# A decoder layer on one core: gathered rows in the output weights' place, and the selection's bias on GpSimd

## The chip, the cores and the metric

The kernel runs on 1 core of one Trainium2 chip. The metric is the device time of one execution in microseconds; before the change it is 1406.47 us, the median of 3 runs (1405.79 to 1407.11).

## The reference, cut to what matters

One layer of a hybrid decoder for 1024 prompt tokens and 32 sample tokens (8 sequences of 4, each with 1024 cached positions), all in float32. All 1056 tokens share the weights.

```
xn   = rms_norm(x);  q, k, v, index q/k/weights = split(xn @ w_in)
a    = sparse attention: score = sum_h iw_h * relu(iq_h . ik); the 256 best keys of each query; softmax over them alone
b    = differential attention: (softmax(q1 k1) - lam * softmax(q2 k2)) @ v
h    = x + concat(a, rms_norm(b) * 0.2) @ w_out
y    = h + MoE(rms_norm(h)):  4 groups x 8 experts; the best group, in it the best 2 experts;
       each expert  (silu(x w_g) * (x w_u) * gate) @ w_d   with w_g, w_u 1024x256 and w_d 256x1024
```

For the sparse attention the kernel must mark for every query exactly 256 keys, with ties at the threshold decided by the lower position, as `top_k` does. For the experts it must add, for each token, two experts' results to `h`.

## The kernel before, in words

The kernel is written with a framework that traces instructions from Python, gives tiles of pools their places, sets all waits, and orders the instructions of each engine by a planner's costs; `mix` interleaves two streams of work by hand-written costs (the numbers that they yield). `V`, `S`, `G`, `T_`, `Y` are VectorE, ScalarE (ACT), GpSimd (POOL), TensorE and SyncE (SP, the queue of plain DMAs). A pool closed and another opened gives its memory on, and a tile of the new pool waits for the tiles that lay in its place (`reuse_waits="tile"`). `tc.issue_after(ins)` puts instructions behind `ins` on its engine.

1. *Projection* (to about 470 us). Six sections of `w_in` on TensorE, each over eight tiles of 128 tokens. Beside it `selection` runs (`score_tile`, `sample_index`, `select`). `select` has seven jobs: query tiles 2 to 7 (widths 384 to 1024) and the 32 sample tokens (width 1056). A bisection and an exact step give each row its threshold `Tv` and the count `need` of entries equal to it that still belong to the 256. Then for each job ACT writes the signs of score minus threshold (L697), VectorE marks the zeros among them (L698), sums them along the row (scan, L699) and compares (L700), which marks what is left out and counts it, and ACT multiplies the marks by 1e30 into the bias tile (L701). `bad` compares the counts with what they should be (L706), and `select_end` has an exact path that is taken only if one differs. The attention reads the bias.
2. *Attention* (to about 920 us), prompt and samples interleaved.
3. *Output projection and routing* (to about 1072 us). `project` multiplies the mixed heads by `w_out`, held as a high and a low part: `woh` and `wol`, 64 KB of each partition on the right side. Its last work on POOL is the power of L1344. `route` finds experts and slots. The list `it0` of an early group, made from what was routed so far, lets experts 0 to 3 begin (`xg0s`, `gu0`, `hid`, `yo0`); the lists `its` of groups 1 to 23 come when all tokens are routed (L1444, L1445).
4. *Experts*. Each group has 128 slots in 4 units of 32 rows; an expert has 96 slots, so it fills three units. For group `g`: `fetch` gathers 128 rows of the stored `h` with an indirect DMA of POOL (L1449); `turn_rows` transposes them on TensorE into two PSUM buffers, which VectorE empties with a multiply (L1458, L1459); `turned_hidden` transposes the hidden rows of the group before (L1478, L1479); `first_products` multiplies by gate and up weights (L1466), four units side by side on TensorE; `gated` applies the silu (L1470, L1472); `down` does the second products of the group before (L1486), ACT writes the result tile `yo` (L1620), and `add_rows` adds it to the output rows with an indirect accumulating DMA of POOL (L1489). Each scatter waits for the one before it, since they write one tensor.

The weights come through SP, in the order of their first use (`weights`, L1253): gate and up together 2 MB (`wg`), down 1 MB (`wd`) for each of 32 experts. There are places for 6 experts of each: four in `xw`, two in `xw2`, which opens in the place of `wol` and the second half of `woh` when the last projection tile begins. A load into a place waits until the products that read it are done. The first load of each kind behind the early ones (`HOLD`) also waits for a copy from `its` on POOL, so that it does not go too early. `ep`, the groups' pool, opens in the place of the routing's pools `fp` and `sm` once these are closed: six row tiles `xg`, each cleared by VectorE before its first gather since a gather skips empty slots, and four result tiles `yo`.

PSUM has eight banks. For the groups `psum(2)` gives two buffers to the transposes (`tr`), two to the first products (`acc`) and two double banks to the second (`S`).

## Time and profile before

| | us |
|---|---|
| median of the runs shown | 1406.47 |
| the profiled execution | 1398.5 |
| its span, first to last instruction | 1396.7 |
| TensorE, VectorE, ACT, POOL busy | 1258.1, 801.4, 561.7, 447.7 |

The page shows the busy share of each engine, the span in slices, and groups of instructions by line. Finer views of the same execution are a timeline by engine, waits by line (who waited for whom, in total), and windows (busy time of each engine in a stretch, with TensorE's granted clock as a share of full speed, the busy share of the DMA engines and the GB/s moved). `PEld` is TensorE's weight load, `SPq` the issue of DMAs on SP; in a timeline the bracket behind a row is the idle time of that engine ahead of it and what ended it. Line numbers are those of the kernel before.

### The profile page before, as it was taken

How to read it: one execution, taken by the hardware profiler on the slowest of the kernel's cores; microseconds unless marked ns; L12 is line 12 of the kernel's file. 1: busy time of each engine (PE TensorE's matmuls, PEld its weight loads, DVE VectorE, ACT ScalarE, POOL GpSimd, SP SyncE). 2: the span in 40 equal slices, each digit the busy share in tenths (PEclk: the TensorE clock that was granted, in tenths of full speed). 3: DMA queues.
4: the chain of work that ended last, by engine and by line, in shares of the span. 5: the costliest groups of instructions: out<-in, count | busy, mean ns of one | idle time of the engine just before them, and what ended most of it. 6: DMA issues, size and time to landing. Idle time of an engine off the chain costs nothing. (4 is left out here: it accounts for less than half of the span.)

```text
span 1396.7 us, 24892 instructions
## 1 busy us (share of the span) xinstructions
PE 1258.1 (90%) x9393; PEld 842.8 (60%) x9393; DVE 801.4 (57%) x2232; ACT 561.7 (40%) x1240; POOL 447.7 (32%) x505
## 2 busy tenths in 40 slices
PE   7999999997789689898889989999998799999994
PEld 5877675875467576675675776768884233333331
DVE  5545996969987677676655556836653311122210
ACT  5533666895432365544445555722221011111110
POOL 1012233254336534335237644322121212222101
PEclk9999999998899799999999999999999899999997
DMA  7223004133325865666558653357636699999962
GB/s 245 68 90 123 25 24 121 48 110 74 99 98 142 233 245 214 232 212 234 178 199 283 222 167 129 92 188 289 248 117 229 235 386 396 396 389 384 391 216 36
DMA packets 114294, 272.60 MB, mean 195 GB/s; under 512 B 52600, under 2 KB 52856, under 8 KB 101880
## 3 DMA queue, kind: packets, MB, share of 16 engines
q1 hardware_dynamic: 81248, 180.84, 35.5%
q0 software_dynamic: 26272, 87.58, 20.0%
q10 hardware_dynamic: 6648, 2.54, 0.7%
q8 instruction: 75, 1.23, 0.3%
q14 instruction: 51, 0.42, 0.1%
HBM read 234.33 MB, written 44.44 MB: 200 GB/s over the span
## 5 line engine op out<-in xcount | busy, mean ns | idle before, releaser
L532 PE MATMUL acc<-wh,xh 128*128 128x512 f32 x432 | 174.6, 404 | 13.8 <-ACT wh L508 13.8
L533 PE MATMUL acc<-wh,xl 128*128 128x512 f32 x432 | 172.0, 398 | 0.0
L1466 PE MATMUL acc<-wg,xT 128*32 128x512 f32 x1472 | 164.3, 598 | 0.0
L941 ACT ACTIVATE mk<-mk,mx 128x256 f32<-128x256 f32 (+7 forms) x128 | 99.0, 774 | 83.2 <-DVE mx L939 78.8
L535 PE MATMUL acc<-wl,xh 128*128 128x512 f32 x320 | 126.5, 395 | 0.0
L1472 DVE SCALAR_TENSOR_TENSOR ac<-acc,its,sg 128x256 f32<-128x256 f32 x23 | 15.8, 688 | 165.1 <-ACT sg L1470 165.1
L532 PEld LDWEIGHTS acc<-wh,xh 128*128 128x128 f32 x432 | 82.5, 191 | 46.3 <-ACT wh L508 22.1
L1466 PEld LDWEIGHTS acc<-wg,xT 128*32 128x32 f32 x1472 | 45.6, 110 | 101.8 <-issue 101.5
L533 PEld LDWEIGHTS acc<-wh,xl 128*128 128x128 f32 x432 | 82.5, 191 | 17.3 <-issue 1.2
L1470 ACT ACTIVATE sg<-acc,its 128x256 f32<-128x256 f32 x23 | 10.9, 473 | 194.7 <-PE acc L1466 194.7
L1486 PE MATMUL S<-wd,aTe 128*32 128x512 f32 x736 | 83.2, 592 | 0.6 <-DVE aTe L1479 0.6
L1105 PE MATMUL tr<-cst,pg 128*128 128x128 f32 x512 | 78.9, 287 | 0.5 <-DVE ql L407 0.4
L937 PE MATMUL tr<-KS,qh 128*128 128x512 f32 (+3 forms) x192 | 74.0, 390 | 1.5 <-DVE aT L865 0.7
L959 POOL TENSOR_SCALAR mk<-mk,rl 128x128 f32<-128x128 f32 (+7 forms) x64 | 49.1, 780 | 69.2 <-DVE rl L951 64.1
L1449 POOL DMA_INDIRECT xg<-s_hn,its x23 | 23.5, 1022 | 140.3 <-PE tr L1458 122.8
L877 PE MATMUL tr<-cst,mk 128*128 128x128 f32 x432 | 64.9, 281 | 3.9 <-POOL mk L959 2.4
L535 PEld LDWEIGHTS acc<-wl,xh 128*128 128x128 f32 x320 | 60.7, 190 | 11.7
L1489 POOL DMA_INDIRECT out_o_y_dram<-yo,its x23 | 36.2, 1576 | 91.7 <-ACT yo L1620 52.1
L1105 PEld LDWEIGHTS tr<-cst,pg 128*128 128x128 f32 x512 | 61.6, 147 | 6.4 <-issue 1.2
L938 PE MATMUL tr<-KS,ql 128*128 128x512 f32 (+3 forms) x192 | 65.1, 353 | 0.0
L1459 DVE TENSOR_TENSOR xT<-tr,gc 128x512 f32<-128x512 f32 x46 | 29.7, 686 | 60.6 <-PE tr L1458 60.6
L877 PEld LDWEIGHTS tr<-cst,mk 128*128 128x128 f32 x432 | 48.5, 142 | 21.8 <-issue 13.5
(447 smaller groups left out, 2913.9 us busy)
## 6 DMA issues: line engine op xcount, KB each, us to landing
wg<-in_w_exp_gate_dram SPq DMA_DIRECT2D x32, 1024.0 KB
wg<-in_w_exp_up_dram SPq DMA_DIRECT2D x32, 1024.0 KB
wd<-in_w_exp_down_dram SPq DMA_DIRECT2D x32, 1024.0 KB
wr<-in_w_in_dram SPq DMA_DIRECT2D x56, 256.0 KB
xt<-in_x_prompt_dram SPq DMA_DIRECT2D x16, 512.0 KB
s_mix<-mo SPq DMA_DIRECT2D x16, 256.0 KB
qn<-s_qa SPq DMA_DIRECT2D x8, 512.0 KB
raw<-in_w_out_dram SPq DMA_DIRECT2D x16, 256.0 KB
```

The source lines that it names most:

```text
L532: T_.matmul(ps, lhsT=xh[t][:, kc, :], rhs=wh[kc], start=kc == 0 and t < NT - 1, stop=False)
L533: T_.matmul(ps, lhsT=xl[t][:, kc, :], rhs=wh[kc], start=False, stop=t == NT - 1 and kc == KC - 1)
L535: T_.matmul(ps, lhsT=xh[t][:, kc, :], rhs=wl[kc], start=False, stop=kc == KC - 1)
L877: T_.transpose(pt[:, (j - b) * P:(j - b + 1) * P], src[:, j * P:(j + 1) * P], ident)
L937: T_.matmul(sp[:, :c1 - c0], lhsT=T.qh[:, h * P:(h + 1) * P], rhs=KS[:, h, c0:c1], start=True, stop=False)
L938: T_.matmul(sp[:, :c1 - c0], lhsT=T.ql[:, h * P:(h + 1) * P], rhs=KS[:, h, c0:c1], start=False, stop=True)
L941: S.activation(mk[:, :W], mk[:, :W], AF.Exp, bias=mx[:, h:h + 1], scale=-1.0, accum_out=T.ll[:, h:h + 1])
L959: G.tensor_scalar(ex[s][:, :W], ex[s][:, :W], T.rl[:, 2 * u + s:2 * u + s + 1], 1.0, op0=ALU.mult, op1=ALU.mult)
L1105: T_.transpose(pt[:, c * P:(c + 1) * P], raws[bb][:, o_:o_ + P], ident)
L1466: T_.matmul(gu[c:c + m, :].rearrange("p (u f) -> p u f", u=2), lhsT=xT[:, k, c:c + m], rhs=wg[:, :, k, :], start=k == 0, stop=k == KC - 1)
L1486: T_.matmul(py[q][c:c + m], lhsT=aT[:, k, c:c + m], rhs=wd[:, k, q * 512:(q + 1) * 512], start=k == 0, stop=k == 1)
L1489: G.indirect_dma_start(out=yd, out_offset=bass.IndirectOffsetOnAxis(ap=it[:, 0:1], axis=0), in_=yo, in_offset=None, compute_op=ALU.add, bo ...
```

## The change

The selection: the zeros among the signs are no longer marked by VectorE; ACT squares the signs (0 for equal, 1 else), and the scan adds a tile of ones and subtracts the squares. The last multiply goes from ACT to GpSimd.

The experts: the row tiles `xg` get a pool of their own, `xg`, on the right side under `xw2`, where the first half of `woh` lay (16 KB, four tiles), open since the last projection tile. The first two are cleared by GpSimd behind the last power, before the lists are known. `ep` keeps two result tiles in place of four, and has a third place for gate and up weights beyond the six. The loads of gate and up of experts 5 and 6 are asked for right behind the first two gathers. `hid` and `yo0` of the early group use another tag of the same pool. PSUM has three buffers for transposes and one for the first products.

```diff
@@ -690,15 +690,18 @@
         V.tensor_reduce(out=need, in_=m8, axis=AX.X, op=ALU.add)
         V.scalar_tensor_tensor(need, ge, 1.0, need, op0=ALU.add, op1=ALU.subtract)
         V.tensor_copy(cnt, thr[:, 2, :nj])
+        unit = sx.tile([P, 1056], BF16, name="unit", bufs=1)
+        G.memset(unit, 1.0)
         V.tensor_scalar(nhi, Tv, -1.0, None, op0=ALU.mult)
         for j, (sc, n, W, bt) in enumerate(J):

             sg, e = junk(), junk()
             S.activation(sg[:n, :W], sc[:n], AF.Sign, bias=nhi[:n, j:j + 1])
-            V.tensor_scalar(e[:n, :W], sg[:n, :W], 0.0, None, op0=ALU.is_equal)
-            V.tensor_tensor_scan(out=e[:n, :W], data0=e[:n, :W], data1=e[:n, :W], initial=0.0, op0=ALU.add, op1=ALU.bypass)
+            S.activation(e[:n, :W], sg[:n, :W], AF.Square)
+
+            V.tensor_tensor_scan(out=e[:n, :W], data0=unit[:n, :W], data1=e[:n, :W], initial=0.0, op0=ALU.add, op1=ALU.subtract)
             V.scalar_tensor_tensor(e[:n, :W], e[:n, :W], need[:n, j:j + 1], sg[:n, :W], op0=ALU.is_gt, op1=ALU.is_gt, accum_out=cnt[:n, j:j + 1])
-            S.mul(bt[:n, :W], e[:n, :W], BIG)
+            G.tensor_scalar(bt[:n, :W], e[:n, :W], BIG, None, op0=ALU.mult)
             yield W * 0.0035

         bad = sx.tile([P, 8], F32, name="bad", bufs=1)
@@ -1242,11 +1245,11 @@
     p4 = ExitStack()
     cq = p4.enter_context(tc.tile_pool(name="cq", bufs=1))
     xw = p4.enter_context(tc.tile_pool(name="xw", bufs=1, reuse_waits="tile"))
-    WG, WD = (4, 6), (4, 6)
+    WG, WD = (4, 6, 7), (4, 6, 6)
     xw2 = []
     NEARLY = ((1, 4), (1, 5), (0, 4))
     HOLD = (1, 1)
-    XG, YO = 6, 4
+    XG, YO = 4, 2
     SPREAD = (1, 1, 2, 3, 4, 4, 6, 6)
     loaded = [0, 0]

@@ -1255,8 +1258,8 @@
         n = loaded[part]
         loaded[part] += 1
         lim = (WG, WD)[part]
-        first = n % lim[1] < lim[0]
-        pool, bufs = (xw, lim[0]) if first else (xw2[0], lim[1] - lim[0])
+        i = n % lim[2]
+        pool, bufs = (xw, lim[0]) if i < lim[0] else (xw2[0], lim[1] - lim[0]) if i < lim[1] else (xw2[2], lim[2] - lim[1])

         def src(nm):
             return a[nm][0, e] if isinstance(e, int) else a[nm][0, bass.ds(e, 1)].rearrange("o k n -> (o k) n")
@@ -1341,7 +1344,9 @@
             st.dma_start(dst[r0:r0 + n], h[:n])
         V.tensor_tensor(out=s1[:n, 0:1], in0=s1[:n, 0:1], in1=s1[:n, 1:2], op=ALU.add)
         V.tensor_scalar(s1[:n, 1:2], s1[:n, 0:1], 1.0 / D, EPS, op0=ALU.mult, op1=ALU.add)
-        G.tensor_tensor(out=s1[:n, 2:3], in0=s1[:n, 1:2], in1=nhalf[:n, 0:1], op=ALU.pow)
+        last_pow[0] = G.tensor_tensor(out=s1[:n, 2:3], in0=s1[:n, 1:2], in1=nhalf[:n, 0:1], op=ALU.pow).ins
+
+    last_pow = [None]

     def route(t, h, s1):

@@ -1542,11 +1547,17 @@

             p3w.close()
             xw2.append(p4.enter_context(tc.tile_pool(name="xw2", bufs=1, side="right", reuse_waits="tile")))
+            xw2.append(p4.enter_context(tc.tile_pool(name="xg", bufs=XG, side="right", reuse_waits="tile")))
             for part, e in NEARLY:
                 W_[(part, e)] = weights(8 * (e % 4) + e // 4, part)
         for part, e in ahead.get(i, ()):
             W_[(part, e)] = weights(8 * e, part)

+    with tc.issue_after(last_pow[0]):
+        xgs = []
+        for _ in range(2):
+            xgs.append(xw2[1].tile([P, D], F32, name="xg"))
+            G.memset(xgs[-1], 0.0)
     step(route_)
     x0T = turn_rows(xg0s[0], lambda: fp.tile([P, KC, P], F32, name="mx"))
     step(route_)
@@ -1578,27 +1589,34 @@
     cnti = cq.tile([P, 2], I32, name="cnti")
     V.tensor_scalar(cnti[:, 0:1], cnt[:, 32:33], float(P - 1 - CAP), None, op0=ALU.add)
     V.tensor_scalar(cnti[:, 1:2], cnti[:, 0:1], 7, None, op0=ALU.arith_shift_right)
-    hid = fp.tile([P, D], F32, name="xt")
+    hid = fp.tile([P, D], F32, name="mh")
     gated(it0[:, 0], gu0, hid[:, :256], hid[:, 256:512])
     aT0 = hid[:, 512:768].rearrange("p (k n) -> p k n", k=2)
     turn_hidden(hid[:, 256:512], aT0)
     py0 = [acc(), acc()]
     second_products(py0, aT0, u0)
-    yo0 = fp.tile([P, D], F32, name="xt")
+    yo0 = fp.tile([P, D], F32, name="mh")
     for q in range(2):
         S.activation(yo0[:, q * 512:(q + 1) * 512], py0[q], AF.Copy, scale=it0[:, 0, 1:2].bitcast(F32))
     p3.close()


-    psum(2)
+    psum(3, 1)
     ep = p4.enter_context(tc.tile_pool(name="ep", bufs=2, reuse_waits="tile"))

     def fetch(it, new=False):
-        xg = ep.tile([P, D], F32, name="xg", bufs=XG)
-        if new:
-            V.memset(xg, 0.0)
+        if xgs:
+            xg = xgs.pop(0)
+        else:
+            xg = xw2[1].tile([P, D], F32, name="xg")
+            if new:
+                G.memset(xg, 0.0)
         fetch_to(it, xg)
         return it, xg
+
+
+    yos = [ep.tile([P, D], F32, name="yo", bufs=YO)]
+    xw2.append(ep)

     def new_xT():
         return ep.tile([P, KC, P], F32, name="xT")
@@ -1616,7 +1634,7 @@
     def down(it, aT, units):
         py = big()
         second_products([py[:, :512], py[:, 512:]], aT, units)
-        yo = ep.tile([P, D], F32, name="yo", bufs=YO)
+        yo = yos.pop() if yos else ep.tile([P, D], F32, name="yo", bufs=YO)
         S.activation(yo, py, AF.Copy, scale=it[:, 1:2].bitcast(F32))
         add_rows(it, yo)

@@ -1638,6 +1656,8 @@
         return units

     fetched = {g: fetch(its[:, g], True) for g in (1, 2)}
+    W_[(0, 5)], W_[(0, 6)] = (weights(8 * (n % 4) + n // 4, 0, its[:, 1, 0:1] if n == 5 else None) for n in (5, 6))
+    held[0] -= 1
     add_rows(it0[:, 0], yo0)
     behind = None
     for g in range(1, NG + 2):
...
```

What is left out at the end are the row tiles of the overflow path, renamed in the same way; that path is not taken here.

## Rows read from the trace of the kernel before

**Rows 1.** The page: engine shares, and TensorE's busy tenths in 40 slices.
```profile
PE 1258.1 (90%) x9393; PEld 842.8 (60%) x9393; DVE 801.4 (57%) x2232; ACT 561.7 (40%) x1240; POOL 447.7 (32%) x505
...
PE   7999999997789689898889989999998799999994
```

**Rows 2.** Windows: length, PE, PEld, DVE, ACT, POOL busy, granted clock, DMA share, GB/s.
```profile
1070.00:1080.00 10.00, 5.48 (x86) 2.10 (x80) 2.08 (x9) 1.85 (x3) 1.47 (x2) 1.00 0.53 211
1080.00:1090.00 10.00, 0.00 (x0) 0.00 (x0) 3.86 (x5) 0.00 (x0) 2.61 (x4) 0.64 0.43 74
1090.00:1100.00 10.00, 8.78 (x60) 3.40 (x64) 3.00 (x4) 0.00 (x0) 4.83 (x5) 0.68 0.70 215
...
1102.00:1340.00 238.00, 230.80 (x2048) 81.18 (x2051) 46.52 (x80) 30.54 (x39) 46.73 (x36) 1.00 1.01 387
```

**Rows 3.** Timeline, all engines, from the slot lists to group 2: start, us, instruction.
```profile
1071.88 0.19 POOL L1272 CAST wg<-its 128x1 f32<-128x1 int32 x1 [10.97 <-DVE its L1445]
...
1074.03 3.64 PE L1486 MATMUL acc<-wd,xt 128*32 128x512 f32 x32 [0.52 <-DVE xt L1479]
...
1078.72 1.71 POOL L1489 DMA_INDIRECT out_o_y_dram<-xt,it  x1 [6.65 <-ACT xt L1589]
1085.49 0.91 DVE L1599 MEMSET xg<- 128x1024 f32 x1 [11.52 <-DMA out_o_y_dram<-xt,it]
...
1087.20 1.06 POOL L1449 DMA_INDIRECT xg<-s_hn,its  x1 [6.78 <-DVE xg L1599]
...
1091.22 1.97 PE L1458 MATMUL tr<-cst,xg 128*128 128x128 f32 x8 [13.55 <-DMA xg<-s_hn,its]
...
1101.74 1.16 PE L1458 MATMUL tr<-cst,xg 128*128 128x128 f32 x8
```

**Rows 4.** Timeline of late groups: transposes, first products, and the readers of `acc`.
```profile
1337.42 0.44 PE L1478 MATMUL tr<-cst,ac 128*128 128x128 f32 x2 [0.34 <-DVE xT L1459]
...
1337.79 7.07 PE L1466 MATMUL acc<-wg,xT 128*32 128x512 f32 x64
...
1345.43 0.68 DVE L1472 SCALAR_TENSOR_TENSOR ac<-acc,its,sg 128x256 f32<-128x256 f32 x1 [7.12 <-ACT sg L1470]
1348.22 1.16 PE L1458 MATMUL tr<-cst,xg 128*128 128x128 f32 x8
...
1362.39 7.07 PE L1466 MATMUL acc<-wg,xT 128*32 128x512 f32 x64
```

**Rows 5.** TensorE's waits from 1100 to 1377: us in total, times, longest.
```profile
PE tr L1478 <- DVE xT L1459: 7.5, 21, 0.8
```

**Rows 6.** Window of the selection's last part, columns as in rows 2.
```profile
340.00:390.00 50.00, 32.19 (x100) 19.27 (x101) 48.07 (x91) 22.68 (x39) 17.24 (x15) 0.77 0.35 92
```

**Rows 7.** TensorE's waits from 340 to 390.
```profile
PE tr L708 <- DVE bad L706: 4.2, 1, 4.2
```

**Rows 8.** POOL's groups of instructions by shape: busy us, mean ns, idle before.
```profile
L959 POOL TENSOR_SCALAR mk<-mk,rl 128x1024 f32<-128x1024 f32 x8 | 8.9, 1120 | 13.1 <-DVE rl L951 8.5 <-PE tr L938 3.1 <-PE tr L877 1.5
...
L1084 POOL MEMSET QB<- 128x1024 f32 x2 | 1.9, 962 | 1.7 <-PE tr L1121 1.7
```

**Rows 9.** POOL's timeline: two scatters in a row in the full stretch.
```profile
1277.51 1.59 POOL L1489 DMA_INDIRECT out_o_y_dram<-yo,its  x1 [0.65 <-issue]
...
1290.81 1.59 POOL L1489 DMA_INDIRECT out_o_y_dram<-yo,its  x1 [1.64 <-DMA out_o_y_dram<-yo,its]
```

**Rows 10.** VectorE's groups of instructions from 340 to 390: the compares.
```profile
L698 DVE TENSOR_SCALAR sjunk<-sjunk 128x384 bf16<-128x384 bf16 (+6 forms) x7 | 4.5, 641 | 0.3 <-ACT sjunk L697 0.3
```

**Rows 11.** VectorE's timeline: two of the compares, of widths 896 and 1024.
```profile
350.06 1.46 DVE L698 TENSOR_SCALAR sjunk<-sjunk 128x896 bf16<-128x896 bf16 x1
...
359.38 0.42 DVE L698 TENSOR_SCALAR sjunk<-sjunk 128x1024 bf16<-128x1024 bf16 x1
```

**Rows 12.** SP's timeline: the first weight load after the pause, and the last.
```profile
1101.85 0.33 SPq L1274 DMA_DIRECT2D wg<-in_w_exp_gate_dram  x1
...
1336.02 0.33 SPq L1267 DMA_DIRECT2D wd<-in_w_exp_down_dram  x1
```

More of the change, by code (lines that the diff above doesn't have):

```diff
@@ L1661, in build @@
         nrow = 32 * OVF
-        ini = ep.tile([P, D], F32, name="xg", bufs=XG)[:, :3 * (nrow // P)].bitcast(I32).rearrange("p (i c) -> p i c", c=3)
+        ini = xw2[1].tile([P, D], F32, name="xg")[:, :3 * (nrow // P)].bitcast(I32).rearrange("p (i c) -> p i c", c=3)
         G.iota(ini[:, :, 0], pattern=[[1, nrow // P]], base=0, channel_multiplier=nrow // P)
         V.tensor_scalar(ini[:, :, 0], ini[:, :, 0], 127, None, op0=ALU.bitwise_and)
-        inif = ep.tile([P, D], F32, name="xg", bufs=XG)[:, :nrow // P]
+        inif = xw2[1].tile([P, D], F32, name="xg")[:, :nrow // P]
         V.tensor_scalar(inif, ini[:, :, 0], float(NTOK), None, op0=ALU.add)
```

## The prediction

> **What bounds the kernel now.** I read the page's engine shares first: TensorE is busy 90% of the span, so time is gained where it stands still or waits, and only there. Its busy tenths in 40 slices of 34.9 us show two dents near the lines of the diff, slices 9 and 10 (counted from 0; about 340 to 390 us) and 30 and 31 (about 1070 to 1100 us), and after them one long full stretch, the expert groups [rows 1]. I cut these stretches into windows, and then read the timeline inside them.
>
> The hole at 1080: in 1070 to 1080 TensorE is busy 5.48 of 10 us, in 1080 to 1090 not at all, and from 1080 to 1100 the granted clock is 0.64 and 0.68 of 2.4 GHz, a mix of its two levels, 1.2 and 2.4 GHz [rows 2]. The timeline says why. The slot lists `its` are done at 1071.88 (they release the POOL cast), but the gather of the first group's rows goes out at 1087.20, since its tile must be cleared first by VectorE (1085.49), in memory that the first result `yo0` still holds until its scatter, issued at 1078.72, has landed. TensorE finishes the early group at 1074.03 + 3.64 = 1077.67 and starts group 1 at 1091.22 [rows 3].
>
> The expert groups after that: from 1102 to 1340 TensorE is busy 230.8 of 238 us and the DMA share is 1.01 at 387 GB/s [rows 2]. Both are full. Which of them ends last is read from the cadence: groups follow each other every 12.30 us without exception, and the only wait that TensorE has in them is one of 0.34 us per group, of the transposes of the hidden rows (L1478) for VectorE to empty a PSUM buffer (L1459), 7.5 us in 21 waits [rows 4, 5]. No wait for weights ends last, so TensorE's own order sets the pace; the weights are near behind.
>
> The selection at 340 to 390: TensorE is busy 32.19 of 50 us there, VectorE 48.07 [rows 6]. VectorE is the bound, and TensorE's last wait in it is 4.2 us for `bad`, the end of the selection [rows 7].
>
> **The change, part by part.**
>
> *A, gathered rows in the output weights' place.* The two first row tiles now lie where the first 16 KB of `woh` lay, whose last reader is the first half of the last tile's projection, and GpSimd clears them after the last power (L1344), in a stretch in which POOL is idle for 10.97 us before the cast [rows 3]. Two GpSimd clears of this size cost 2 x 0.96 us [rows 8], hidden in that idle time; without that cover they would cost 1.9. The gathers can then go right after the cast, at 1072.1. A gather on a lightly used DMA took 1091.22 - 1087.20 = 4.0 us; the dearest nearest row is a scatter in the full stretch, 1277.51 to 1290.81 = 13.3 us [rows 3, 9]. At 1072 one 2 MB weight load (expert 5's, which that cast releases) runs beside it, a state near the light end, so I take 7 us: landed at 1079. TensorE is free at 1077.67, so group 1 starts at 1079 in place of 1091.22: 12.2 us. Group 1 before, from its first transpose to the next group's, took 1101.74 - 1091.22 = 10.5 us, at the lower clock; a later group, which also transposes hidden rows, takes from 1335.9 (12.30 before 1348.22) to the end of its first products, 1337.79 + 7.07 = 1344.9, 8.9 us, or 8.0 without the 0.34 and about 0.5 for that transpose [rows 3, 4]. With a pause of 1.3 us in place of 13.6 I expect the clock to stay up: 2.5 us more. A = 14.7 us; bounds 16.0 (no pause) and 5.8 (a 13.3 us gather, slow clock as before).
>
> What queues behind: on POOL the scatter of `yo0` follows the two gathers, is ready only at 1078, and waits for neither. On SP the two gate/up loads of experts 5 and 6 stand ahead of all others; the one for 6 goes to a new third place that lies over `yo0`, so it blocks SP until about 1086, but the next load could not go before the first products of group 1 release a place, at about 1087. It costs nothing.
>
> *B, PSUM.* `psum(3, 1)` gives the transposes a third buffer and takes one from the first products. The hidden transposes no longer wait for the buffer of L1459 and run inside the time in which the first products wait for that same evacuation anyway. 0.34 us per group, 21 times, is 7.5 us [rows 4, 5]. The first products have one buffer now: it is free when VectorE's L1472 ends (1345.43 + 0.68), and is wanted after the next row transposes, 1348.22, so 2.1 us stay in hand [rows 4]. The late one next is the evacuation L1459 itself, which the products need. B = 7.5, bounds 0 and 7.5.
>
> *C, the selection.* Out: seven compares on VectorE, 4.5 us in all. ACT's seven multiplies go to GpSimd; ACT gets seven squares of the same widths in their place, so its sum stays, and its waits for VectorE go [rows 10]. The scan and the final compare stay on VectorE, on the same number of inputs. GpSimd gets seven multiplies; a one-input multiply of 128x1024 f32 took it 1.12 us, so at most 7.8 us, and one clear [rows 8]. They hide in POOL's idle time, but VectorE, which is full, pays where the two get in each other's way: the compare of 128x896 took 1.46 us and the wider one of 128x1024 0.42 [rows 11]. Bounds: +4.5 us if nothing collides, 4.5 - 7.8 = -3.3 if VectorE stands still for every one of the multiplies. The slow compare shows that collisions happen, the quick one that they are not the rule; I put half of 7.8 against 4.5 and take C = 1 (0.6, and a little for the casts of ACT that no longer stand behind its waits).
>
> The Trainium skill speaks against this part: "SBUF — State Buffer", section "Who interferes with whom", says that VectorE with two SBUF inputs and GpSimd reading SBUF exclude each other for the whole instruction. By it the scan, the final compare and most of the section's own VectorE work collide with each multiply, and the sum would be 20 in place of 23; the two compares agree that something blocks, not that it always does.
>
> *D, the rest.* Two result buffers in place of four: the scatter of a group must have landed before ACT writes two groups later, 24.6 us on; the dearest seen is 13.3 [rows 9]; nothing, while they do not pile up. Four row tiles in place of six: each gather still has some 37 us of lead. A third place beyond the six for gate/up weights lets expert 6 load before group 1 is done: the first request after the pause was at 1101.85, the last at 1336.02, 78 loads of 1 MB [rows 12].
>
> **Sum.** 14.7 + 7.5 + 1 = 23.2 us. The profiled execution took 1398.5 us (span 1396.7), so 1375.3 by its own time. The median shown, 1406.47, is 8.0 us above it; the parts are times of single stages, so I take them off the median as they are: 1383.3 us.
>
> **The rivals.**
>
> 1. *The weights bind.* For: the DMA share is 1.01 [rows 2], and TensorE now wants everything 14.7 to 22 us earlier. The 78 loads need some 240 us from the first request at full rate. From about 1087 they would end at about 1330; the last group's first products, at 1362.39 before [rows 4], would begin at about 1340. Some 10 us stay in hand by this, less in the middle, where TensorE's part of B is not yet gained but the row traffic of the faster groups (they gather and scatter sooner) takes its share. If they bind, TensorE follows the stream and B is lost with a little more: a gain of 13 to 18, about 1391.
> 2. *The gather goes late*, behind the scatter of `yo0`, or shares badly with the weight load: start at 1085.4, gain 5.8 + 7.5 + 1 = 14.3, 1392.
> 3. *The third transpose buffer brings nothing*, because VectorE's order or the single product buffer puts the same wait elsewhere: 15.7, 1390.8.
> 4. *The lock of the shared port* makes C -3.3 (this is what the skill's rule would give at its worst): gain 18.9, 1387.6.
> 5. *Slower: the scatters pace the groups.* Scatters into the same output follow one another, each waiting for the one before, and with two buffers ACT, then PSUM, then TensorE stand behind them. At 13.3 us each, 22 groups would take 22 x 1.0 us longer than now, B would be gone, and the result is 1406.5 - 14.7 - 1 + 22 = 1412.8. For: 13.3 is above the cadence of 12.30. Against: POOL waited just 1.64 us for it there [rows 9]. It turns slower when a scatter takes 12.30 + 15.7 / 22 = 13.0 us on average.
>
> **How the numbers follow.** My forecast has 0.45; rival 1 0.15, rival 2 0.12, rival 3 0.08, rival 4 0.08; several together that leave under 2.8 us (0.2%, about what a measurement of this kernel can tell from no change) 0.05; rival 5, or an order of the whole that turns out worse, 0.07. So faster 0.88, same 0.05, slower 0.07. The low end: A at 16.0, B 7.5, C 4.5 and some 2 us of luck in the order, 30 off: 1376. The high end holds rivals 1 to 4 and two of them together (a late gather and C at its worst, without B: 2.5 to 6 us off): 1400.
>
> **What would show it.** A: the gather of group 1 within 2 us of the cast, its row transposes within 3 us of the end of the early group, and a granted clock near 1.00 from there on. B: a cadence of 11.96 us and no wait of L1478 for L1459. C: VectorE's stretch from the first Sign to `bad` shorter than before, and TensorE's 4.2 us wait there smaller. Wrong: waits of L1466 for a weight load (rival 1), of ACT's L1620 for a scatter (rival 5), POOL's multiplies with the VectorE scans stretched to match (rival 4).

## The result, and the profile after

The changed kernel takes 1397.32 us (median of 4 runs, 1394.7 to 1398.63) against 1406.79 for the kernel before on the same chip (4 runs, 1405.79 to 1408.61): ratio 0.9931, 95% interval 0.9909 to 0.9954, so 9.5 us faster. I forecast 1383.3, a gain of 23.2: the time lies inside the range of 1376 to 1400, but only 9.5 of the 23.2 us came.

The first profile of before took 1398.5 us, 8 us under its own median; that of after took 1398.63. So the two spans, 1396.7 and 1396.8, hide the gain, and the traces have to be compared stage by stage. The page of after, as in [rows 1] (engine: busy us, share; then TensorE's busy tenths):

```profile
PE 1267.7 (91%) x9393; PEld 906.9 (65%) x9393; DVE 795.9 (57%) x2219; ACT 562.5 (40%) x1240; POOL 473.5 (34%) x517
...
PE   7999999996799689898889989999999899999994
```

The dent in slices 30 and 31 is gone, the one in slice 9 is deeper. Windows against [rows 2] (here only length, PE, granted clock, DMA share, GB/s): TensorE, which stood still from 1080 to 1090, is now busy 7.87 us there, and the stream is as full as before.

```profile
1070.00:1080.00 10.00, 7.68 (x51) 0.86 0.88 341
1080.00:1090.00 10.00, 7.87 (x100) 0.84 0.27 77
1090.00:1100.00 10.00, 8.98 (x80) 0.96 0.82 241
1102.00:1340.00 238.00, 232.00 (x2046) 0.99 1.02 390
```

The timeline from the clears to group 1 answers to [rows 3] (routing lines stand 5 higher: L1449 is L1454, L1458 is L1463, L1466 is L1471):

```profile
1069.45 3.67 DVE L1436 TENSOR_SCALAR b<-b,cst 128x2 f32<-128x2 f32 x1
1069.48 1.83 POOL L1560 MEMSET xg<- 128x1024 f32 x2
1069.58 3.54 DVE L1464 TENSOR_TENSOR mx<-tr,gc 128x512 f32<-128x512 f32 x1
1071.26 1.84 POOL L1613 MEMSET xg<- 128x1024 f32 x2
1073.15 0.16 DVE L1437 TENSOR_TENSOR b<-b,ov 128x2 f32<-128x2 f32 x1
...
1084.16 0.20 DVE L1450 COPY its<-low 128x48 f32<-128x48 f32 x1
1085.03 1.11 POOL L1454 DMA_INDIRECT xg<-s_hn,its  x1 [11.94 <-DVE cnti L1591]
1086.47 5.34 PE L1491 MATMUL acc<-wd,mh 128*32 128x512 f32 x32 [0.52 <-DVE mh L1484]
1091.73 1.16 PE L1463 MATMUL tr<-cst,xg 128*128 128x128 f32 x8
1093.92 0.68 PE L1463 MATMUL tr<-cst,xg 128*128 128x128 f32 x4 [1.02 <-DMA xg<-s_hn,its]
```

Two things are to be seen. The gather goes out 0.9 us after the lists, and group 1 starts right behind the early group: 7.6 us after the lists, where it took 19.6. But the lists themselves are late. All four clears run on GpSimd in the last tile's routing, and for just as long VectorE's next step, 128x2 elements, takes 3.67 us (the same line takes 0.21 to 0.23 at all other times).

Late in the groups, against [rows 4, 5]: the wait of the hidden transposes is gone and the cadence is 12.06 to 12.14 us (it was 12.30), until group 21.

```profile
1331.86 1.16 PE L1463 MATMUL tr<-cst,xg 128*128 128x128 f32 x8
1332.86 0.38 PE L1483 MATMUL tr<-cst,ac 128*128 128x128 f32 x2
1333.40 1.06 PE L1471 MATMUL acc<-wg,xT 128*32 128x512 f32 x6 [0.16 <-issue]
1336.13 8.32 PE L1471 MATMUL acc<-wg,xT 128*32 128x512 f32 x57 [1.67 <-SPq L1680]
1348.24 1.16 PE L1463 MATMUL tr<-cst,xg 128*128 128x128 f32 x8
```

TensorE stops after 6 of 64 first products, and the group lasts 1348.24 - 1331.86 = 16.4 us: 4.3 of the gain go there. The releaser named is SP's branch of the overflow test (L1680), which moves no data, so what it waited for was open.

### The profile page after: what moved, and what is told of

Its sections match the earlier page's. It is cut to its first block, busy times and chain, and to the rows that moved or that the text cites. A ratio compares the mean times of both kernels' runs of the same rounds, so it can differ in the third digit from the quotient of the medians.

```text
span 1396.8 us, 24901 instructions
## 1 busy us (share of the span) xinstructions
PE 1267.7 (91%) x9393; PEld 906.9 (65%) x9393; DVE 795.9 (57%) x2219; ACT 562.5 (40%) x1240; POOL 473.5 (34%) x517
## 5 line engine op out<-in xcount | busy, mean ns | idle before, releaser
L1471 PE MATMUL acc<-wg,xT 128*32 128x512 f32 x1472 | 167.6, 598 | 5.7 <-DVE xT L1464 2.9
L1471 PEld LDWEIGHTS acc<-wg,xT 128*32 128x32 f32 x1472 | 83.9, 110 | 73.8 <-issue 59.0
L532 PEld LDWEIGHTS acc<-wh,xh 128*128 128x128 f32 x432 | 83.1, 192 | 48.0 <-ACT wh L508 23.2
L1491 PE MATMUL S<-wd,aTe 128*32 128x512 f32 x736 | 86.8, 592 | 0.6 <-DVE aTe L1484 0.6
L1454 POOL DMA_INDIRECT xg<-s_hn,its x23 | 23.8, 1033 | 153.5 <-PE tr L1483 133.7
L1491 PEld LDWEIGHTS S<-wd,aTe 128*32 128x32 f32 x736 | 44.4, 110 | 34.9 <-issue 32.9
```

Of the source, the lines that this page charges most:

```text
L532: T_.matmul(ps, lhsT=xh[t][:, kc, :], rhs=wh[kc], start=kc == 0 and t < NT - 1, stop=False)
L1471: T_.matmul(gu[c:c + m, :].rearrange("p (u f) -> p u f", u=2), lhsT=xT[:, k, c:c + m], rhs=wg[:, :, k, :], start=k == 0, stop=k == KC - 1)
L1491: T_.matmul(py[q][c:c + m], lhsT=aT[:, k, c:c + m], rhs=wd[:, k, q * 512:(q + 1) * 512], start=k == 0, stop=k == 1)
```

## The experiments

Each kernel was timed in five rounds beside the kernel before on one chip; a gain is (1 - ratio) times the median of before. The chips differ (medians of before 1377.9, 1405.1, 1405.4 and 1379.3 us in the four groups), so kernels are compared by their medians within a group, or by their gains across groups. Across groups 2 us say little: the kernel after itself gained 9.7 us on one chip (by its ratio) and 7.6 on another (r5).

My theory after the two traces: the clears cost 3.5 us, the third transpose buffer half of what I forecast, the selection 1 to 2, and the 7 us that the attention stage seemed to lose between the traces are scatter. Rivals: the selection slows what stands behind it; and for the stop in group 21, an accident of one execution, or late weights.

**r1, the kernel before again.** No edit.

> The kernel before, unchanged, against itself. Both theories expect 0 in the times. They differ in the profile. Theory 1 (the first profiled execution of before, 1398.5 us, was a quick one, 8 us under its own median, so the 7 us that the attention stage between 430 and 1060 us seems to lose between the two traces are an accident of that execution): the new profile is nearer to 1406, and the first transpose of group 1 stands 5 to 9 us later than at 1091.22. Theory 2 (the change itself slows the attention stage by 7 us through the selection): the new profile again has group 1 near 1091 whenever its span is near 1397, and the extra time of the timed runs lies elsewhere, in the expert groups for instance.

Ratio 1.0006 (0.9993 to 1.0018). On this chip group 1's transposes begin at 1068.88, 22 us earlier than in the first profile, and all of that arises from 530 to 890 us, the attention stage. Its scatter between executions and chips is larger than any part of this change. The test I had written (near 1406 or not) can't be read on such a chip; theory 2 falls by r2 and r3. Nor is the cadence of the kernel before always 12.30 us: here group 18 takes 12.63, of which more below.

**r2, the experts' part alone**, and **r3, the selection alone.**

```diff
# r2: after, with the compares, scan and S.mul of before (L697 to L704)
# r3: before, with the squares, scan and G.tensor_scalar of after
```

> The kernel after with the old selection (compares on VectorE, bias on ScalarE). Theory 1 (selection costs 1 to 2 us, the rest of the change brings 9.5 less 1 to 2): 10 to 12 us faster than before, 1.0 to 2 us faster than the kernel after. Theory 2 (the selection is what slows the stage behind it by 7 us): 16 to 18 us faster than before.

> The kernel before with the new selection alone (squares on ScalarE, bias on GpSimd). Theory 1: 1 to 2 us slower than before (my forecast of the step was 1 faster); VectorE's stretch from the first Sign to `bad` as long as in the kernel after. Theory 2: 6 to 8 us slower. The rule of the shared port at its worst: 3.3 slower.

r2: 0.9915 (0.9897 to 0.9933), 11.7 us faster. r3: 1.0020 (1.0006 to 1.0035), 2.8 slower. The parts add up, 11.7 - 2.8 = 8.9. The selection loses, a little more than theory 1 said and far less than theory 2. In r2 TensorE stops in groups 18, 19 and 21, 5.9 us together, and two of the three waits name a load (us in total, times, longest):

```profile
PE acc L1468 <- DMA wg<-in_w_exp_up_dram: 1.8, 2, 1.2
PE acc L1468 <- SPq L1677: 1.4, 1, 1.4
```

**r4, two transpose buffers again.**

```diff
-    psum(3, 1)
+    psum(2)
```

> The kernel after with two transpose buffers and two buffers of the first products again, as before the change. Theory (the third buffer brings 0.17 to 0.18 us per group, 21 times): 3.6 to 4 us slower than the kernel after, 5 to 6 us faster than before, with a cadence of 12.30 us and the wait of the hidden transposes for VectorE back. By the forecast's size (0.34 per group) it would be 7.5 slower than after. A rival, that the weights pace the groups in any case (cadence 12.1 because the loads bind): no difference to the kernel after.

0.9923 (0.9906 to 0.9939), 10.6 us faster than before: with two buffers the kernel is not slower than after (9.7 by its ratio and, in r5, 7.6). On the same chip it is 2.1 us slower than r2 by the medians, less than the 2.8 that its selection alone costs (r3), so the third buffer gives nothing here. The cadence is 12.30, the hidden transposes wait 7.2 us again, and no group stops: from the third on all take 12.3 us. What the third buffer gives is taken back; the rival, that the weights pace the groups, has it.

**r5, the kernel after again; r6, clears on ScalarE; r7, half of the late down loads; r8, r6 with the old selection.**

```diff
# r6, r8 (two before ScalarE's L1374, two after its L1390)
-            G.memset(xgs[-1], 0.0)
+            S.activation(xgs[-1], hs[t][0], AF.Copy, scale=0.0)
# r7, in weights(), part 1
+            if n >= 12:
+                Y.dma_start(w[:, 0:1], src("w_exp_down")...[:, 0:1])
+                return w[:, 0:1].to_broadcast([P, 2, D])
```

> The kernel after, unchanged, to be compared with the others of this group. 8 to 11 us faster than before. The two theories of the stall near the end (weights late, or an instruction fetch) differ in the profile: if the weight stream binds, TensorE again loses 3 to 6 us between groups 17 and 21, in waits of the first products for gate or up weights, at a place that shifts from run to run; if it was an accident of one execution, the cadence stays at 12.1 us to the end and the kernel is 4 us faster than its first profile.

> The kernel after with the four clears of the gathered rows on ScalarE (a copy scaled by 0) in place of GpSimd. Theory (GpSimd's clears stop VectorE for 3.5 us in the last tile's routing, which is on the path): VectorE's 128x2 step of L1436 back from 3.67 to about 0.2 us, slot lists 2.3 to 3.8 us earlier, and since the held weight loads start with the lists, 2 to 4 us faster than the kernel after at the end. Rival (the stream of weights sets the end whatever TensorE does before): lists earlier, but under 1 us at the end. Rival (the 3.67 us are the wait for something else, such as PSUM or a semaphore): lists not earlier.

> The kernel after, but from the 13th load of down weights on only the first half of each is loaded and used twice, so the second half of those down products is wrong: some 8 MB, about 21 us of the stream at 387 GB/s, are left out. Theory (the weights bind near the end, so a faster TensorE only waits for them): no stall in groups 17 to 21, 3 to 6 us faster than the kernel after; the cadence stays near 12.1 us. Rival (the stall is an instruction fetch or TensorE's own): within 1 us of the kernel after.

> The clears on ScalarE and the old selection together, with the rest of the change: the best kernel if the theories hold. 14 to 17 us faster than before (11.7 for the change without its selection, and 2 to 4 for the clears); if the weights set the end, 11 to 13.

r5: 0.9946 (0.9929 to 0.9963), 7.6 us faster than before, and TensorE stops in groups 18, 19 and 21, 4.7 us together. r7: 0.9912 (0.9885 to 0.9940), 7.0 us faster than r5 by the medians (the intervals overlap a little), and no stop: the cadence is 12.06 to 12.15 us to the last group. It leaves out 20 halves of 0.5 MB, so 10 MB, not the 8 that I wrote. So the stops go when the weights come sooner; that they are waits for a load is shown below by the load's own landing.

r6: 0.9918 (0.9899 to 0.9938), 4.2 us faster than r5 by the medians. VectorE's step is short again, and the lists come 4.0 us earlier against the work before them (1078.81 and 1080.83, while the projection stands 2.0 us later):

```profile
1066.27 1.99 ACT L1560 ACTIVATE xg<-xt 128x1024 f32<-128x1024 f32 x2
1068.01 0.22 DVE L1436 TENSOR_SCALAR b<-b,cst 128x2 f32<-128x2 f32 x1
1078.81 0.20 DVE L1450 COPY its<-low 128x48 f32<-128x48 f32 x1
1084.69 1.16 PE L1463 MATMUL tr<-cst,xg 128*128 128x128 f32 x8
1089.36 0.69 PE L1463 MATMUL tr<-cst,xg 128*128 128x128 f32 x4 [3.50 <-DMA xg<-s_hn,its]
1089.97 8.74 PE L1471 MATMUL acc<-wg,xT 128*32 128x512 f32 x64
```

The fifth row is new: with three transpose buffers the planner sets half of group 2's transposes ahead of group 1's products, and TensorE waits there for group 2's gather (1.02 us in after, 3.50 here). r8: 0.9903 (0.9884 to 0.9923), 13.6 us faster (13.1 by the medians), below what I expected; it stops in group 21 for 1.6 us and waits 3.1 for that gather.

**Which load.** A group has four units and an expert fills three, so the last unit of group 18 is the first of expert 25 (counted in the order of loading), and the last of group 21 the first of expert 29, whose up half is the third last up load. TensorE stops after 6 products, which are those of the three other units. From the issue of that load to the moment at which TensorE goes on in group 21:

| kernel | third last up load issued | first products resume | apart |
|---|---|---|---|
| after | 1311.97 | 1336.13 | 24.16 |
| r2 | 1279.11 | 1303.28 | 24.17 |
| r5 | 1308.39 | 1332.56 | 24.17 |
| r6 | 1308.08 | 1332.28 | 24.20 |
| r8 | 1304.27 | 1328.45 | 24.18 |
| r9 (below) | 1303.36 | 1328.13 | 24.77 |

The trace of r2 also has the time of that load itself, 24.1 us from issue to landing, so at 1303.2, and TensorE goes on at 1303.28 (SP's timeline, TensorE's, and the DMA issues, whose last column is the landing time):

```profile
1279.11 0.33 SPq L1274 DMA_DIRECT2D wg<-in_w_exp_up_dram  x1
...
1303.28 6.62 PE L1468 MATMUL acc<-wg,xT 128*32 128x512 f32 x57 [1.37 <-SPq L1677]
```
```profile
wg<-in_w_exp_up_dram SPq DMA_DIRECT2D x1, 1024.0 KB, 24.1
```

Now the kernel before. Its first profile has no landings, but that of r1, the same kernel, has those of expert 25's up half and of expert 29's:

```profile
1252.73 0.46 SPq L1274 DMA_DIRECT2D wg<-in_w_exp_up_dram  x1
...
1278.75 7.40 PE L1466 MATMUL acc<-wg,xT 128*32 128x512 f32 x64
...
1291.35 0.33 SPq L1274 DMA_DIRECT2D wg<-in_w_exp_up_dram  x1
...
1315.98 7.07 PE L1466 MATMUL acc<-wg,xT 128*32 128x512 f32 x64
```
```profile
wg<-in_w_exp_up_dram SPq DMA_DIRECT2D x1, 1024.0 KB, 26.3
wg<-in_w_exp_up_dram SPq DMA_DIRECT2D x1, 1024.0 KB, 23.5
```

Expert 25's half lands at 1252.73 + 26.3 = 1279.0, after group 18 has begun its products (1278.75) and 0.2 us before the one that reads it (1279.22); these products take 7.40 us in place of 7.07. Expert 29's lands at 1291.35 + 23.5 = 1314.9, 1.1 us before group 21 begins its products. In the first profile the same load was issued here:

```profile
1312.96 0.33 SPq L1274 DMA_DIRECT2D wg<-in_w_exp_up_dram  x1
```

With 23.5 to 24.2 us it landed at 1336.5 to 1337.2 (an estimate); group 21's first products began at 1337.79 [rows 4]. The stream was about 1 us ahead of TensorE in the kernel before, not 10, and in group 18 it could already be late. In r3, whose experts' part is that of before, TensorE stops there:

```profile
1283.68 6.60 PE L1469 MATMUL acc<-wg,xT 128*32 128x512 f32 x57 [0.31 <-DMA wg<-in_w_exp_up_dram]
```

Group 18 takes 12.63, 13.62 and 12.94 us in r1, r3 and r12, the groups around it 12.30. Only the first profile, from which I predicted, has 12.30 there too.

**r9, the third gate/up place earlier; r10, with group 2's transposes behind group 1's products; r11, r10 with two transpose buffers; r12, before with squares and ScalarE's multiply.** In after, the third place lies over `mh`, where `yo0` waits for its scatter, and its load stands at the head of SP's queue until that has landed (r5, SP's timeline and SP's waits; the first row holds the gate loads of experts 5 and 6, and lasts until the second, the one of the third place, has been issued, 12.96 us). Nothing else is issued meanwhile:

```profile
1084.36 12.96 SPq L1277 DMA_DIRECT2D wg<-in_w_exp_gate_dram  x2
1097.37 0.52 SPq L1277 DMA_DIRECT2D wg<-in_w_exp_up_dram  x1
```
```profile
SPq L1277 <- DMA out_o_y_dram<-mh,it: 10.9, 1, 10.9
```

```diff
# r9, on r8
-    hid = fp.tile([P, D], F32, name="mh")
+    hid = fp.tile([P, D], F32, name="xt")      # yo0 the same
# r10, on r9
-            xT = turn_rows(xg, new_xT)
+            with tc.issue_after(last_first[0]) if g == 2 else ExitStack():
+                xT = turn_rows(xg, new_xT)      # last_first: the last first product issued
# r11, on r10
-    psum(3, 1)
+    psum(2)
# r12, on r3
-            G.tensor_scalar(bt[:n, :W], e[:n, :W], BIG, None, op0=ALU.mult)
+            S.mul(bt[:n, :W], e[:n, :W], BIG)
```

> The kernel of r8 (clears on ScalarE, old selection) with the early group's hidden rows and its result in the two `xt` buffers as before the change, so that the third gate/up place lies over tiles that are free when the early group's first products end. Expert 6's gate/up load (2 MB, 5.4 us of the stream at 387 GB/s) then no longer stands at the head of the SP queue for some 12.9 us until the scatter of `yo0` has landed. Theory (the weights bind, and TensorE's late stalls are the stream's lag behind group 1's start): the load is issued within 3 us of the slot lists, the late stall (1.6 us in r8's profile, 4.7 in r5's) is gone, and the kernel is 1.5 to 4 us faster than r8's 13.1 us gain: 14.5 to 17 us faster than before. Rival (the extra load delays the gathers of groups 1 and 2 by as much as it gains): 11 to 13.5 us faster.

> r9 with one more line: the row transposes of group 2 may not be issued before the last first product of group 1. With three transpose buffers the planner puts half of them ahead of group 1's products, where TensorE waited 3.1 us for group 2's gather in r8's profile. Theory: that wait is gone and group 2's rows are there 9 us later anyway, so 2 to 3.5 us faster than r9 if the weights no longer bind, 0 to 1 if they still do.

> r10 with two transpose buffers and two of the first products. In the kernel after, r4 gave the same time with two as with three. Theory (a faster cadence only ran into the weights there): with the weights 2 MB further ahead, two buffers are now 2 to 4 us slower than r10, at a cadence of 12.30 us against 12.12. Rival (the third buffer is worth nothing even with weights in hand): within 1 us of r10.

> The kernel before with the squares and the scan of the new selection, but the multiply by the bias on ScalarE as before (ScalarE then makes three passes, sign, square and multiply, and GpSimd none). Theory (GpSimd's multiplies are what VectorE pays for; without them VectorE saves its compares, 4.5 us): 1 to 4 us faster than before, 4 to 7 faster than the selection of r3 (which was 2.8 slower than before). Rival (the new scan itself, with two different inputs, or the wait for ScalarE's squares is what costs): as slow as r3, 2 to 4 us slower than before.

r9: 0.9888 (0.9858 to 0.9919), 15.7 us faster, 2.1 more than r8 on another chip, which is within the scatter of gains. SP is blocked 2.27 us in place of 12.96, and the load's up half leaves 5.9 us after the lists (1083.85 and 1077.94), not within 3. The stop did not go: group 21 stops again, and loses 4.7 us. r10: 0.9868 (0.9841 to 0.9895), 18.6 us faster, 2.7 better than r9 by the medians (the intervals overlap), without a stop: its third last up load was issued at 1301.08 and its group 21 begins the products at 1328.40, 27.3 us later, so some 3 in hand by the table's 24.2 (an estimate). It is not much: in r16, the same kernel, expert 30's up half lands 0.7 us before the product of group 22 that reads it. r11: 0.9884 (0.9856 to 0.9912), 16.3 faster: here, with the weights in time, two buffers lose 2.0 us by the medians, though the intervals overlap, so the times alone don't decide; in the profiles the cadence is 12.30 against 12.06 to 12.14. r12 missed: 1.0022 (1.0003 to 1.0040), 3.1 us slower where I expected a gain.

**r13 to r16, the selections on the best kernel.** r16 is r10 unchanged; r13 has the selection of the change, r14 that of r12, r15 the old compares with the multiply on GpSimd.

```diff
# r15, on r10
-            S.mul(bt[:n, :W], e[:n, :W], BIG)
+            G.tensor_scalar(bt[:n, :W], e[:n, :W], BIG, None, op0=ALU.mult)
```

> The kernel of r10 with the new selection as in the change (squares on ScalarE, bias on GpSimd). In the profiles of before and after, the stretch from the thresholds to `bad` is 42.8 us with the old selection, 43.8 with the new one. Theory 1 (the new selection costs the stage 1 to 2 us through GpSimd's multiplies, and the rest seen in r3 was scatter of the attention stage): 1 to 2 us slower than r10's kernel. Theory 2 (the 2.8 us of r3 are real, whatever base): 2.5 to 3.5 slower.

> The kernel of r10 with squares, scan and multiply as in r12 (ScalarE three passes, GpSimd none). In r12's profile the stretch to `bad` is 40.5 us, 2.3 shorter than with the old selection, yet r12 was 3.1 us slower than before. Theory 1 (the stage sets it, r12's loss was scatter of the attention stage): 0.5 to 2.5 us faster than r10's kernel. Theory 2 (something behind `bad` is later, ScalarE's extra pass delaying the casts of the projection, or another order of the attention): 1 to 3 us slower.

> The kernel of r10 with the old compares on VectorE and only the bias multiply moved to GpSimd. Theory 1 (GpSimd's multiplies stop VectorE: 43.8 - 40.5 = 3.3 us of the stretch in r3 against r12): the stretch to `bad` 45 to 46.5 us, 2.5 to 4 us slower than r10's kernel, the worst of the four selections. Rival (VectorE is not held, the multiplies only end late): within 1 us of r10's.

> The kernel of r10, unchanged, as the measure for r13 to r15: 16 to 19 us faster than before. If the weights still set the end in some executions, a stall of 2 to 5 us in group 21 comes back in this profile, ending about 5 to 7 us after the last up load was issued, as in r5 and r9; r10's own profile had none.

| | thresholds to `bad`, us | TensorE at 437 against 335 us, to r16 | median | ratio to before |
|---|---|---|---|---|
| r16 old | 42.8 | 0 | 1357.82 | 0.9842 (0.9818 to 0.9865) |
| r13 new | 43.1 | +1.7 | 1361.00 | 0.9872 (0.9851 to 0.9892) |
| r14 ScalarE | 40.5 | -0.4 | 1358.95 | 0.9855 (0.9833 to 0.9876) |
| r15 GpSimd's multiply alone | 45.3 | +2.8 | 1362.91 | 0.9878 (0.9858 to 0.9897) |

The third column is the shift of the same matrix products behind the selection, less their shift ahead of it. The stretch to `bad` adds up: the squares shorten it by 2.3 us (r14), GpSimd's multiply lengthens it by 2.5 (r15), both together by 0.3 (r13). The order is that of theory 1, r15 the worst, as expected; r14 is no gain. r13's 3.2 us in the median and r15's 5.1 are more than the 1.7 and 2.8 of the stage; where the rest arises was not followed. GpSimd's multiplies in after, of 128x384, 640 and 896, 512, 1024, 768:

```profile
347.46 1.56 POOL L704 TENSOR_SCALAR bias<-sjunk 128x384 bf16<-128x384 bf16 x1 [3.47 <-DVE sjunk L703]
352.19 6.47 POOL L704 TENSOR_SCALAR bias<-sjunk 128x640 bf16<-128x640 bf16 x2 [1.44 <-DVE sjunk L703]
359.97 3.48 POOL L704 TENSOR_SCALAR bias<-sjunk 128x512 bf16<-128x512 bf16 x1 [0.78 <-DVE rsq L351]
365.44 3.16 POOL L704 TENSOR_SCALAR bias<-sjunk 128x1024 bf16<-128x1024 bf16 x1
370.50 2.58 POOL L704 TENSOR_SCALAR bias<-sjunk 128x768 bf16<-128x768 bf16 x1 [1.05 <-DVE rsq L351]
```

Without them `bad` comes 2.3 us earlier (r14), but TensorE's other waits of this stretch then grow: ScalarE has a third pass to make, and the casts `wh` that it owes TensorE come later. The same wait from 340 to 395 us in r16 and in r14:

```profile
PE acc L532 <- ACT wh L508: 14.9, 3, 9.5
PE tr L708 <- DVE bad L706: 4.2, 1, 4.2
```
```profile
PE acc L532 <- ACT wh L508: 19.0, 5, 9.5
PE tr L711 <- DVE bad L709: 3.2, 1, 3.2
```

## Why the prediction was wrong

**The stream (the step that failed).** I put rival 1 aside with "Some 10 us stay in hand by this", and gave it 0.15. That sum compared the end of all loads with the last group, and took the time of the requests ("some 240 us"; 1101.85 to 1336.02 is 234) for the end of the loads. A load lands some 24 us behind its request, and in r1 the last up load is in 252.5 us after the first request (1079.71 to 1332.2), which takes the 10 us away. And what counts is each group's own load: group 21's was about 1 us early in the kernel before, group 18's 0.2 us (r1). I also let the stream begin at "about 1087", 8 us after group 1's start. Before, it begins when group 1's first products free a place, 10.6 us after the start (1101.85 - 1091.22). In after the first load into a freed place leaves 9.9 us after it (1101.63 - 1091.73), in r5 11.3 (1097.99 - 1086.72), behind expert 6's. So starting group 1 earlier moved the stream with it by about as much, and A's gain was kept; anything that TensorE gained behind that had to be waited for. The load that decides was issued 241.3 us after the lists before (1312.96 - 1071.67) and 227.8 after (1311.97 - 1084.16): 13.5 us. From the lists to the end of the span it is 325.0 us before (327.4 and 326.3 in r1 and r3, which have the same experts' part), 312.6 in after and 310.4 in r5: a gain of 12.4 to 17.0 where A and B were to bring 22.2. Rival 1's sum, 13 to 18 with B lost, was the right one for this stretch.

**A.** The mechanism and its size held: lists to group 1's transposes 19.6 before, 7.6 in after, 5.9 in r5, so 12.0 to 13.7 us where I wrote 12.2. The gather took 4.1 to 4.5 us where its landing is recorded (r2, r4, r13 to r15), not 7, and TensorE came free last. The 1.7 us between after and r5 are the early group's second products: 5.34 us in after, with a granted clock of 0.50, the lower level, from 1088 to 1090, when TensorE had been busy 2.3 of the 4 us to 1086; 3.64 in r5, at 1.00. Group 1 itself ran as forecast, at the full clock. Its transposes took 1.16 us in place of 1.97 and its first products 7.07 in place of 8.69, 2.4 us less (before, then after):

```profile
1093.12 8.69 PE L1466 MATMUL acc<-wg,xT 128*32 128x512 f32 x64
1094.53 7.07 PE L1471 MATMUL acc<-wg,xT 128*32 128x512 f32 x64
```

But half of group 2's transposes stood between the two and took part of it back (in after 0.68 us and 1.02 of waiting), so group 1's products ended 0.7 (after) to 1.3 us (r5) sooner, counted from its start, not 2.5. In r4 and r10, which don't have that order, group 1 takes 8.5 us in place of 10.5.

What failed in A is the price of the clears, "hidden in that idle time; without that cover they would cost 1.9". I looked at GpSimd's idle time only. They stop VectorE, which is on the path to the lists, for 3.5 us. r6 shows it: the same clears on ScalarE, and the lists come 4.0 us earlier. From the last product of the projection to the lists it is 14.4 us in every kernel without GpSimd's clears, and with them 16.7 (r2, r7) to 18.4 (after, r4, r5). In the latter three TensorE, which behind the stop was busy for 1.7 of 4 us, ran the next 4 us at a granted clock of 0.57 to 0.68, a mix of both levels; in r2 and r7, busy 1.8 and 1.7 of 4, it kept 1.00. The Trainium skill has this rule on the page I had read for part C ("SBUF — State Buffer", section "Who interferes with whom"): a `tensor_scalar` of VectorE may use both of its port pairs, one of which is GpSimd's, and then waits while GpSimd holds it. The trace agrees, with 3.67 us for a step of 0.22. I weighed the page against the selection and not against the clears.

**B.** The wait of [rows 5] went, as said, but the cadence fell by 0.19 us, not 0.34, so 4 us in 21 groups in place of 7.5: the first products now wait 0.20 for the evacuation of the rows (2.9 us in 14 times), which the wait had hidden, and the second products take 3.72 to 3.76 in place of 3.62 us; why they do was not tried. In after these 4 us brought nothing, by the stream (r4); with the weights in time about 2 us by the medians (r10 against r11, the intervals overlap).

**C.** Forecast 1 us of gain, measured 2.8 of loss (r3), 1.7 of it in the stage (r13). Both terms of the sum were off: leaving out the compares shortened the stretch to `bad` by 2.3 us, not 4.5 (r14 against r16), and the multiplies lengthened it by 2.5 (r15 against r16), where I had put 3.9. I took GpSimd's multiply from 128x1024 f32, 1.12 us [rows 8], as an upper bound; in this stretch, beside a busy VectorE, 128x1024 bf16 took 3.16, 128x512 3.48. (The "20" that I gave by the page's rule and rival 4's 18.9 should be one number; C = -3.3 gives 18.9.) And the two compares of [rows 11] did not show that collisions are not the rule: GpSimd ran a product beside the slow one, at 350.06, and was idle beside the quick one, at 359.38:

```profile
349.55 1.72 POOL L340 TENSOR_TENSOR m<-raw,gtab 128x512 f32<-128x512 f32 x1 [4.85 <-ACT raw L377]
356.45 0.46 POOL L176 TENSOR_TENSOR gtab<-rot,g 128x128 f32<-128x128 f32 x1 [5.18 <-DVE raw L342]
362.90 1.04 POOL L387 TENSOR_TENSOR outl<-outl,rk 128x512 f32<-128x512 f32 x1 [5.99 <-DVE rk L385]
```

What I left out altogether: TensorE waits some 14 us for ScalarE's casts in this stretch (13.8 before, 14.9 in r16), and less than 5 for `bad`, so the end of VectorE's work was not the only thing that counts. How r12 loses 3.1 us with a shorter stretch was not found; r14, the same selection on another kernel, is within 1.1 us of r16.

**D.** Result buffers and row tiles cost nothing, as said. The third place blocked SP longer than "until about 1086": in r5 until 1097.0, 1.0 us after group 1's first products had ended (1095.98). So it cost the stream about 1 us there (an estimate), none in after, where it was free before they ended. It also gave little: its own load left only 1.0 (r5) to 2.3 us (after) before the next.

The sum by what was measured: 12.4 to 17.0 from the lists to the end, less 4.0 for the clears, less 1.7 to 2.8 for the selection: 5.6 to 11.3. The timed gains are 9.7 and 7.6. That the time lies inside the range is luck: it is rival 1 in the groups, a loss in the selection, and the clears, which no rival had. (Two rivals together, from which I drew the high end, give by their own figures 2.5 to 6 us off, so up to 1404 and not 1400.)

The version to keep is r10: clears on ScalarE, the old selection, three transpose buffers, `hid` and `yo0` in `xt`, group 2's transposes in their turn: 0.9868 (0.9841 to 0.9895) and again, as r16, 0.9842 (0.9818 to 0.9865), 18.6 and 21.8 us faster than before, on two chips. By r16's 0.7 us its weights land just in time, so a still faster TensorE would probably wait for them again (not tried).

## What to carry to other kernels

Two resources that are both full can both be critical: before a gain on one is counted, take the load that a late group waits for, add its measured time from issue to landing, and see how long before its use it lands. Do it in more than one profile: of the four with the old experts' part (the first, r1, r3, r12) only the first has an even cadence in group 18. Work moved to an idle engine is free only if it takes nothing that a busy engine needs; look at who runs beside it, not at the idle time of the engine that gets it.

## What the runs showed of the hardware

- Four GpSimd clears in a row, 3.6 us, held one VectorE step of 128x2 f32 for 3.67 us, not for one clear alone; the next instruction, with one input from PSUM, stood behind it. ScalarE did the same clears in 4.0 us and stopped nobody.
- In the full stretch a 1 MB weight load lands long after its issue: the up halves from expert 12 on took 15.5 to 31.0 us in the eight traces that record landings (r1 to r4 and r13 to r16, two chips), though 1 MB at 387 GB/s is 2.7 us. At least five earlier loads were still on their way when r2 issued expert 29's up half, which took 24.1.
- The same program takes 1378 and 1379 us on two chips, 1405 on two others; between the profiles of before and r1 the same matrix products stand 0.7 us earlier at 530 us, 22.8 at 890 and 21.8 at the end: it arises in the attention stage, where cache rows are gathered by index. What in it differs was not tried.
